# The last LayerNorm of a DiT layer: the second tile's mean taken off in PSUM by TensorE, its root by ScalarE's Sqrt and one Newton round

## The chip, the cores and the metric

The kernel runs on one core of a Trainium2 chip, in fp32 with products split into high and low parts. A core has five engines that run side by side and wait for each other through semaphores: TensorE (PE in the profile, with its weight loads as PEld), VectorE (DVE), ScalarE (ACT), GpSimd (POOL) and SyncE (SP), which here issues the DMAs. Each engine works its own instructions off in order. The metric is the device time of one execution in microseconds (us), as the median of several runs.

## What is computed

One layer of a diffusion transformer: 256 latent tokens and 256 context tokens of width 2048, two groups of attention heads, one output projection, a SwiGLU feed-forward network of width 5632, and a LayerNorm behind each of the two residual sums. Cut to its end, which is what the change concerns:

```python
def layer_norm(x, g, b):
    xf = x.astype(jnp.float32)
    mu = jnp.mean(xf, axis=-1, keepdims=True)
    var = jnp.mean(jnp.square(xf - mu), axis=-1, keepdims=True)
    return ((xf - mu) * lax.rsqrt(var + EPS) * g + b).astype(x.dtype)
...
x = layer_norm(DN_ALPHA * x + g1 * (heads @ w_out[layer]), ln1_g[layer], ln1_b[layer])
x = layer_norm(DN_ALPHA * x + g2 * swiglu(modulate(x, sh2, sc2), w_gate[layer], w_up[layer], w_down[layer]),
               ln2_g[layer], ln2_b[layer])
```

## The kernel before

The 256 latent tokens are two tiles t = 0, 1 of 128 tokens, one token to a partition. `xt[:, t, :]` holds the 2048 features of a tile, worked on in four blocks n = 0..3 of 512 columns, as wide as one PSUM bank. There are eight banks, four in the pool "acc" and four in the pool "wk".

A weight block (128 rows x 4 x 512 columns) is loaded by SP into a `raw` tile, cast by ACT into a high part `hi` (L331), and DVE subtracts to get the low part `lo` (L332). PE then does three products for every block of 128 rows (L341 to L343, `mm3`). The `hi`/`lo` pieces stand in four buffers, so ACT's next cast waits until PE has done with an older piece. Most of the kernel's order on each engine is decided by a scheduler at build time; inside `tc.manual_schedule` the code's own order holds for the named engines.

The end of the kernel is the down projection, block by block of output columns. For each block n < 3, `residual` (L1197) multiplies the sum by the gate, adds it to `xt` and takes its statistics with bn_stats (L1201). For the last block, `last_steps` (L1875) puts the gate into the last three weight groups instead (L1891, `gated`), adds what the earlier groups gave to `xt` (L1899, L1900, `seed`), copies that into a PSUM bank (L1901), and lets PE add the last three groups on top of it, for tile 0 first and then for tile 1. So the bank `whole[t]` ends up with the finished residual sum of block 3.

Then comes `ending(t, ps)` (L1833), in its own order on DVE and ACT. It takes bn_stats of the bank, calls `ln_scalars(t, True)` (L1203), which merges the four statistics (L1206) and finds one over the root of the variance: a first guess by shifting bits (L1210, L1211, L1213 on DVE) and three Newton rounds on ACT (L1216 to L1218). Meanwhile DVE takes off the mean and multiplies by the gain in all four blocks (L1826, `first_step`). When the root is there, DVE multiplies by it and adds the bias (L1830, `last_step`), and each piece goes out by a DMA on SP's queue (L1831). Tile 1's block 3 is cut into 384 and 128 columns.

Other names: `l2g` and `l2b` are the LayerNorm's gain and bias, spread over the partitions and loaded long before the end; `ident` is a 128x128 identity, `ones` a 128x128 matrix of ones, `bcol` a tile of bias columns, all three last read well before the end; `stats`, `mv` (mean, variance), `lv`, `la`, `ly` are the small tiles of the statistics.

Of the kernel before, what the change touches and what calls it, by code (L numbers as in the profile page):

```python
# [13 lines left out]
F32 = mybir.dt.float32  # L14
# [4 lines left out]
AF = mybir.ActivationFunctionType  # L19
ALU = mybir.AluOpType  # L20
# [3 lines left out]
P = 128  # L24
# [4 lines left out]
NT = SEQ // P  # L29
# [4 lines left out]
EPS = 1e-6  # L34
SCALE = HD ** -0.5
ALPHA = 2.0 ** 0.25
NB = 512
# [229 lines left out]
def dit_layer(ctx: ExitStack, tc: tile.TileContext, x, c, cx, c_ctx, w_ada, b_ada, w_in, q_norm_g,  # L267
              k_norm_g, sink_logit, w_out, ln1_g, ln1_b, w_gate, w_up, w_down, ln2_g, ln2_b,
              rope_cos, rope_sin, out):
    nc = tc.nc  # L270
    x, c, cx = x[0], c, cx[0]
    w_ada, w_in, w_out, w_gate, w_up, w_down = (w[0] for w in (w_ada, w_in, w_out, w_gate, w_up, w_down))

    main = ctx.enter_context(tc.tile_pool(name="main", bufs=1))
# [5 lines left out]
    def acc_bank():  # L280
        return acc_ps.tile([P, NB], F32, tag="acc", name="acc")

    def wk_bank():
        return wk_ps.tile([P, NB], F32, tag="wk", name="wk")
# [14 lines left out]
    ident = main.tile([P, P], F32, tag="ident", name="ident")  # L299
    make_identity(nc, ident)  # L300
    fill(main, 416)
    xt = main.tile([P, NT, D], F32, tag="xt", name="xt")
    stats = main.tile([P, NT, 4, 6], F32, tag="stats", name="stats")
# [4 lines left out]
    def load_raw(w, k0, nk, c0, width):  # L308
        raw = raw_tile()
        rv = raw[:, : nk * width]  # L310
        nc.sync.dma_start(
            rv.rearrange("p (k n) -> p k n", k=nk),
            w[k0 * P : (k0 + nk) * P, c0 : c0 + width].rearrange("(k p) n -> p k n", p=P),
        )
        return rv

    def load_split(w, k0, c0, nk=G4, width=NB, spare=False):
        return split_raw(load_raw(w, k0, nk, c0, width), spare)

    def split_raw(raw, spare=False):  # L320

        parts = []
        for s in range(0, raw.shape[-1], SUB * NB):
            n = min(SUB * NB, raw.shape[-1] - s)
            if spare:
                both = wraw.tile([P, 2, SUB * NB], F32R, tag="raw", name="hilo")
                hi, lo = both[:, 0, :], both[:, 1, :]
            else:
                hi = whl.tile([P, SUB * NB], F32R, tag="hi", name="hi")
                lo = whl.tile([P, SUB * NB], F32R, tag="lo", name="lo")  # L330
            nc.scalar.copy(hi[:, :n], raw[:, s : s + n])  # L331
            nc.vector.tensor_tensor(lo[:, :n], raw[:, s : s + n], hi[:, :n].bitcast(F32), op=ALU.subtract)  # L332
            parts += [(hi[:, j : j + NB], lo[:, j : j + NB]) for j in range(0, n, NB)]
        return parts
# [5 lines left out]
    def mm3(ps, xh, xl, w, first, last, seeded=False):  # L340
        nc.tensor.matmul(ps, lhsT=xh, rhs=w[0], start=first, stop=False, skip_group_check=seeded)  # L341
        nc.tensor.matmul(ps, lhsT=xh, rhs=w[1], start=False, stop=False, skip_group_check=seeded)  # L342
        nc.tensor.matmul(ps, lhsT=xl, rhs=w[0], start=False, stop=last, skip_group_check=seeded)  # L343
# [67 lines left out]
    ones = main.tile([P, P], F32, tag="ones", name="ones")  # L411
# [3 lines left out]
    bcol = main.tile([P, 6 * KD], F32, tag="bcol", name="bcol")  # L415
# [787 lines left out]
    def ln_scalars(t, beside=False):  # L1203

        mv = main.tile([P, 2], F32, tag="mv", name="mv", bufs=2)
        nc.vector.bn_aggr(mv, stats[:, t, :, :])  # L1206
        v = main.tile([P, 2], F32, tag="lv", name="lv", bufs=2)
        y = main.tile([P, 1], F32, tag="ly", name="ly", bufs=2)
        a = main.tile([P, 1], F32, tag="la", name="la", bufs=2)
        nc.vector.tensor_scalar_add(v[:, 0:1], mv[:, 1:2], EPS)  # L1210
        nc.vector.tensor_single_scalar(a.bitcast(I32), v[:, 0:1].bitcast(I32), 1, op=ALU.logical_shift_right)  # L1211
        (nc.scalar.mul if beside else nc.vector.tensor_scalar_mul)(v[:, 1:2], v[:, 0:1], -0.5)
        nc.vector.tensor_scalar(y.bitcast(I32), a.bitcast(I32), -1.0, float(0x5F3759DF), op0=ALU.mult, op1=ALU.add)  # L1213
        for i in range(3):
            if beside:
                nc.scalar.activation(a, y, AF.Square)  # L1216
                nc.scalar.activation(a, a, AF.Copy, bias=1.5, scale=v[:, 1:2])
                nc.scalar.activation(y, y, AF.Copy, scale=a)  # L1218
            else:
                nc.vector.tensor_scalar(a, y, y, v[:, 1:2], op0=ALU.mult, op1=ALU.mult)  # L1220
                nc.vector.tensor_scalar(y, a, 1.5, y, op0=ALU.add, op1=ALU.mult)
        return mv[:, 0:1], y

    norm = {}
# [70 lines left out]
    start = F.add("SP", 0, lambda: None, at=1e5)  # L1295
# [3 lines left out]
    for g in range(last):  # L1299
        n = GROUPS[g][1]  # L1300
# [493 lines left out]
    whole = pb.tile([P, NT, NB], F32, tag="lgb", name="hh")  # L1794
# [15 lines left out]
    l2g, l2b = l2[:, 0, :], l2[:, 1, :]  # L1810
# [13 lines left out]
    def first_step(t, n, ps):  # L1824
        sl = slice(n * NB, (n + 1) * NB)
        nc.vector.scalar_tensor_tensor(xt[:, t, sl], xt[:, t, sl] if n < 3 else ps, norm[t][0], l2g[:, sl], op0=ALU.subtract, op1=ALU.mult)  # L1826

    def last_step(t, n, s, width):
        sl = slice(n * NB + s, n * NB + s + width)
        nc.vector.scalar_tensor_tensor(xt[:, t, sl], xt[:, t, sl], norm[t][1], l2b[:, sl], op0=ALU.mult, op1=ALU.add)  # L1830
        nc.sync.dma_start(out[0, t * P : (t + 1) * P, sl], xt[:, t, sl])  # L1831

    def ending(t, ps):  # L1833
        nc.vector.bn_stats(stats[:, t, 3, :], ps)
        norm[t] = ln_scalars(t, True)
        for n in range(4):
            first_step(t, n, ps)
        for n in range(4):
            if n < 3 or t == 0:
                last_step(t, n, 0, NB)  # L1840
            else:
                last_step(t, n, 0, 3 * P)
                last_step(t, n, 3 * P, P)

    def share(n, e):

# [28 lines left out]
    def last_steps():  # L1875

        n, ng = 3, KF // G4
        sl = slice(n * NB, (n + 1) * NB)
        whole = [acc_bank() for _ in range(NT)]
        raws, ws = {}, {}  # L1880

        def mms(ps, g, t):
            for j in range(4):
                k = g * 4 + j
                mm3(ps, hTh[g][:, j, t * P : (t + 1) * P], hTl[g][:, j, t * P : (t + 1) * P], ws[g][j],
                    False, k == KF - 1 or k == (ng - TAIL) * 4 - 1, True)

        def gated(g):
            raws[g] = load_raw(w_down, g * 4, G4, n * NB, NB)
            wv = raws[g].rearrange("p (k n) -> p k n", k=G4)  # L1890
            nc.vector.tensor_mul(wv, wv, g2sb[:, None, sl].to_broadcast([P, G4, NB]))  # L1891

        def step(g):
            ws[g] = load_split(w_down, g * 4, n * NB)
            for t in range(NT):
                mms(accs[n][t], g, t)

        def seed(t):
            nc.vector.tensor_mul(yts[t], accs[n][t], g2sb[:, sl])  # L1899
            nc.vector.tensor_add(xt[:, t, sl], xt[:, t, sl], yts[t])  # L1900
            nc.scalar.copy(whole[t], xt[:, t, sl])  # L1901

        def tail():
            g0 = ng - TAIL
            gated(g0)
            step(g0 - 1)
            ws[g0] = split_raw(raws[g0])
            gated(g0 + 1)
            seed(0)
            gated(g0 + 2)  # L1910
            ws[g0 + 1] = split_raw(raws[g0 + 1])
            ws[g0 + 2] = split_raw(raws[g0 + 2], True)
            seed(1)
            for t in range(NT):
                for g in range(g0, ng):
                    mms(whole[t], g, t)
            with tc.manual_schedule(engines={ET.DVE, ET.Activation}):
                for t in range(NT):
                    ending(t, whole[t])

        return [lambda g=g: step(g) for g in range(ng - TAIL - 1) if g != FOLD_H] + [tail]

# [63 lines left out]
```

## Time and profile before

| | us |
|---|---|
| median of 3 runs | 1124.48 |
| lowest and highest run | 1122.33, 1124.83 |
| span of the profiled execution, first to last instruction | 1121.0 |
| PE's weight loads busy, share of the span | 79% |
| largest group: L341 to L343 into acc, u2h and u2l, 3 x 390 products | 456 |
| casts of weights on ACT (L331), 279 of them | 290.7 |
| low parts of weights on DVE (L332), 279 of them | 336.1 |

The profile is of one execution; it gives the span and no time outside of it, so the medians and the span are not the same measure. In its rows stand the start and the length in us, the engine, the line of the code, the operation, output and inputs by the program's names (buffer numbers left out), their shapes, and how many instructions are merged in the row; in brackets stands how long the engine had idled and what it waited for. In rows of groups the line comes first, and behind the shapes the count, the busy time in us and the mean length of one in ns.

### The profile page before, as it was taken

What the parts mean: (1) busy time and instruction counts of PE and PEld (TensorE: products, weight loads), DVE (VectorE), ACT (ScalarE), POOL (GpSimd) and SP (SyncE); (2) the same over time, 40 slices, a digit from 0 to 9 for tenths busy, and PEclk for the clock granted to TensorE, in tenths of its full rate; (3) what the DMA queues carried; (4) which work ended last, traced back from release to release, by engine and by line L of the source; (5) the groups of instructions that cost most, each with busy time, mean ns of one, the idle gap of its engine ahead of it and who ended that gap; (6) DMA issues with size and microseconds to landing.
All of it is one profiled execution on the core that took longest, in us unless ns stands there. A gap on an engine that the chain in (4) does not pass through costs nothing.

```text
span 1121.0 us, 14130 instructions
## 1 busy us (share of the span) xinstructions
PE 1102.3 (98%) x5213; PEld 883.7 (79%) x5213; DVE 903.4 (81%) x1133; ACT 598.7 (53%) x875; POOL 36.7 (3%) x82
## 2 busy tenths in 40 slices
PE   8999999999999999999999999999999999999995
PEld 6766688777887788888888878888888888888884
DVE  5763589899999888787778697988996987689876
ACT  3341554878685356444475565767766344444442
POOL 1000030110100001000000000000000000000000
PEclk9999999999999999999999999999999999999998
DMA  9999999778999778999956677777776998669742
GB/s 321 394 385 375 393 362 377 247 234 274 345 332 395 249 269 321 348 318 296 336 182 216 223 220 266 234 246 271 228 267 216 329 348 293 228 235 379 287 149 76
DMA packets 178317, 321.26 MB, mean 287 GB/s; under 512 B 8732, under 2 KB 43196, under 8 KB 175943
## 3 DMA queue, kind: packets, MB, share of 16 engines
q1 hardware_dynamic: 177528, 320.03, 81.7%
q8 instruction: 41, 0.67, 0.2%
q10 hardware_dynamic: 720, 0.33, 0.1%
q14 instruction: 28, 0.23, 0.1%
HBM read 304.07 MB, written 16.25 MB: 286 GB/s over the span
## 4 chain that ended last, share of the span: by engine, by line
PE 91%; DMA 3%; DVE 2%; ACT 1%; SPq 1%; issue 0%; ACTq 0%; DVEq 0%
PE acc L341 20%; PE acc L343 20%; PE acc L342 20%; PE wk L342 8%; PE wk L341 8%; PE wk L343 8%; PE wk L1081 2%; PE wk L654 2%; DMA raw<-in_w_in_dram 2%; DVE lo L332 1%; DMA lgb<-in_ln_g_dram 1%; PE wk L755 1%; SPq L569 1%; DMA xt<-in_x_dram 0%; PE wk L1414 0%
## 5 line engine op out<-in xcount | busy, mean ns | idle before, releaser
L331 ACT CAST hi<-raw 128x1024 fp32r<-128x1024 f32 x279 | 290.7, 1054 | 256.4 <-PE acc L343 162.4
L332 DVE TENSOR_TENSOR lo<-raw,hi 128x1024 fp32r<-128x1024 f32 x279 | 336.1, 1220 | 103.6 <-ACT hi L331 101.4
L341 PE MATMUL acc<-hi,u2h 128*128 128x512 f32 x390 | 152.5, 391 | 0.0
L343 PE MATMUL acc<-hi,u2l 128*128 128x512 f32 x390 | 151.7, 390 | 0.7 <-DVE u2l L1669 0.7
L342 PE MATMUL acc<-lo,u2h 128*128 128x512 f32 x390 | 151.8, 389 | 0.0
L603 ACT CAST hi<-raw 128x1024 fp32r<-128x1024 f32 (+1 forms) x86 | 87.4, 1030 | 113.8 <-DMA raw<-in_w_in_dram 63.2
L466 DVE SCALAR_TENSOR_TENSOR adav<-raw,cs,adav 128x512 f32<-128x512 f32 (+1 forms) x128 | 121.4, 949 | 8.4 <-DMA raw<-in_w_ada_dram 4.9
L606 DVE TENSOR_TENSOR lo<-raw,hi 128x1024 fp32r<-128x1024 f32 (+1 forms) x86 | 101.3, 1194 | 16.3 <-ACT hi L603 15.5
L341 PE MATMUL acc<-hi,uh 128*128 128x512 f32 x256 | 103.7, 405 | 1.3 <-ACT uh L769 0.8
L342 PE MATMUL wk<-lo,u2h 128*128 128x512 f32 x264 | 103.1, 390 | 0.5 <-DVE lo L332 0.5
L343 PE MATMUL wk<-hi,u2l 128*128 128x512 f32 x264 | 102.7, 389 | 0.0
L341 PE MATMUL wk<-hi,u2h 128*128 128x512 f32 x264 | 102.2, 389 | 0.0
L342 PE MATMUL acc<-lo,uh 128*128 128x512 f32 x256 | 100.5, 392 | 0.6 <-DVE lo L606 0.6
L343 PE MATMUL acc<-hi,ul 128*128 128x512 f32 x256 | 100.1, 391 | 0.4 <-DVE ul L784 0.4
L341 PE MATMUL acc<-hi,hTh 128*128 128x512 f32 x236 | 92.0, 390 | 0.4 <-ACT acc L1901 0.4
L342 PE MATMUL acc<-lo,hTh 128*128 128x512 f32 x236 | 91.8, 389 | 0.0
L343 PE MATMUL acc<-hi,hTl 128*128 128x512 f32 x236 | 91.8, 389 | 0.0
L343 PEld LDWEIGHTS acc<-hi,u2l 128*128 128x128 f32 x390 | 73.2, 188 | 16.2 <-DVE u2l L1669 1.1
L341 PEld LDWEIGHTS acc<-hi,u2h 128*128 128x128 f32 x390 | 73.2, 188 | 16.1 <-ACT u2h L1668 0.8
L342 PEld LDWEIGHTS acc<-lo,u2h 128*128 128x128 f32 x390 | 73.2, 188 | 15.1
L341 PEld LDWEIGHTS acc<-hi,uh 128*128 128x128 f32 x256 | 48.1, 188 | 19.0 <-issue 5.6
L342 PEld LDWEIGHTS wk<-lo,u2h 128*128 128x128 f32 x264 | 49.5, 188 | 12.0 <-DVE lo L332 1.8
(277 smaller groups left out, 1748.0 us busy)
## 6 DMA issues: line engine op xcount, KB each, us to landing
raw<-in_w_ada_dram SPq DMA_DIRECT2D x70, 1024.0 KB, 7.7
raw<-in_w_gate_dram SPq DMA_DIRECT2D x44, 1024.0 KB, 6.7
raw<-in_w_up_dram SPq DMA_DIRECT2D x44, 1024.0 KB, 5.6
raw<-in_w_down_dram SPq DMA_DIRECT2D x44, 1024.0 KB, 5.8
raw<-in_w_ada_dram SPq DMA_DIRECT2D x48, 512.0 KB, 5.9
raw<-in_w_in_dram SPq DMA_DIRECT2D x18, 1024.0 KB, 11.0
raw<-in_w_out_dram SPq DMA_DIRECT2D x16, 1024.0 KB, 6.5
pd<-hx SPq DMA_DIRECT2D x64, 128.0 KB, 3.4
```

What stands on the lines that cost most here:

```text
L331: nc.scalar.copy(hi[:, :n], raw[:, s : s + n])
L332: nc.vector.tensor_tensor(lo[:, :n], raw[:, s : s + n], hi[:, :n].bitcast(F32), op=ALU.subtract)
L341: nc.tensor.matmul(ps, lhsT=xh, rhs=w[0], start=first, stop=False, skip_group_check=seeded)
L342: nc.tensor.matmul(ps, lhsT=xh, rhs=w[1], start=False, stop=False, skip_group_check=seeded)
L343: nc.tensor.matmul(ps, lhsT=xl, rhs=w[0], start=False, stop=last, skip_group_check=seeded)
L466: nc.vector.scalar_tensor_tensor(a[:, c : c + piece], raw[:, f : f + piece], cs[:, 4 * (g * (G4 * NB // w) + j) + 2, None], a[:, c : c + p ...
L569: nc.sync.dma_start(room.t, w[k0 * P : (k0 + 1) * P, c0 : c0 + width])
L603: nc.scalar.copy(hl.hi[:, :n], raw.t[:, s : s + n])
L606: nc.vector.tensor_tensor(hl.lo[:, :n], raw.t[:, s : s + n], hl.hi[:, :n].bitcast(F32), op=ALU.subtract)
L654: nc.tensor.matmul(bank.t[32 * j : 32 * j + 32, :width], lhsT=cs[:, 4 * k + 2 - 2 * i : 4 * k + 34 - 2 * i], rhs=raw.t[:, c * width : (c + ...
L755: nc.tensor.transpose(ps.t[:, (j * 2 + t) * P : (j * 2 + t + 1) * P], src, ident)
L1081: nc.tensor.matmul(o_ps.t[:, : 2 * P].rearrange("p (g q) -> p g q", q=32), lhsT=v, rhs=pv[:, k], start=k == 0, stop=k == 3)
```

## The change

For tile 1, the three blocks that are finished early (n = 0, 1, 2) are multiplied by the gain ahead of time and put into three banks of the "wk" pool (`scaled_tokens`). When the mean is known, ACT makes a diagonal matrix of minus the mean (the identity was negated earlier), and PE adds minus mean times gain to each of the three banks. Only block 3 still has its mean taken off by DVE. The root comes from ACT's Sqrt with a table that is loaded earlier, a reciprocal on DVE and one Newton round there; minus half the variance is made on POOL. The last steps of the three blocks read the banks, block 3 goes first, and the cut into 384 and 128 columns moves to block 2. Tile 0 stays as it was.

```diff
-    def last_step(t, n, s, width):
+    def last_step(t, n, s, width, src=None):
         sl = slice(n * NB + s, n * NB + s + width)
-        nc.vector.scalar_tensor_tensor(xt[:, t, sl], xt[:, t, sl], norm[t][1], l2b[:, sl], op0=ALU.mult, op1=ALU.add)
+        src = xt[:, t, sl] if src is None else src[:, s : s + width]
+        nc.vector.scalar_tensor_tensor(xt[:, t, sl], src, norm[t][1], l2b[:, sl], op0=ALU.mult, op1=ALU.add)
         nc.sync.dma_start(out[0, t * P : (t + 1) * P, sl], xt[:, t, sl])
...
         for n in range(4):
-            if n < 3 or t == 0:
-                last_step(t, n, 0, NB)
-            else:
-                last_step(t, n, 0, 3 * P)
-                last_step(t, n, 3 * P, P)
+            last_step(t, n, 0, NB)
+
+    eps = bcol[:, 0:1]
+
+    def scaled_tokens(t):
+        res = [wk_bank() for _ in range(3)]
+        for n, q in enumerate(res):
+            nc.vector.tensor_mul(q, xt[:, t, n * NB : (n + 1) * NB], l2g[:, n * NB : (n + 1) * NB])
+        nc.scalar.mul(ident, ident, -1.0)
+        nc.gpsimd.memset(eps, EPS)
+        nc.scalar.activation(bcol[:, 1:2], stats[:, t, 2, 2:3], AF.Sqrt, bias=eps)
+        return res
+
+    def last_ending(t, ps, scaled):
+        mv, lv, ly, la = (main.tile([P, w], F32, tag=c, name=c, bufs=2) for c, w in (("mv", 2), ("lv", 2), ("ly", 1), ("la", 1)))
+        nc.vector.bn_stats(stats[:, t, 3, :], ps)
+        nc.vector.bn_aggr(mv, stats[:, t, :, :])
+        nc.gpsimd.tensor_scalar(lv[:, 0:1], mv[:, 1:2], -0.5, -0.5 * EPS, op0=ALU.mult, op1=ALU.add)
+        nc.scalar.activation(ones, ident, AF.Copy, scale=mv[:, 0:1])
+        nc.scalar.activation(lv[:, 1:2], mv[:, 1:2], AF.Sqrt, bias=eps)
+        for n, q in enumerate(scaled):
+            nc.tensor.matmul(q, lhsT=ones, rhs=l2g[:, n * NB : (n + 1) * NB], start=False, stop=True, skip_group_check=True)
+        norm[t] = mv[:, 0:1], ly
+        first_step(t, 3, ps)
+        nc.vector.reciprocal(ly, lv[:, 1:2])
+        nc.vector.tensor_scalar(la, ly, ly, lv[:, 0:1], op0=ALU.mult, op1=ALU.mult)
+        nc.vector.tensor_scalar(ly, la, 1.5, ly, op0=ALU.add, op1=ALU.mult)
+        last_step(t, 3, 0, NB)
+        for n in range(2):
+            last_step(t, n, 0, NB, scaled[n])
+        last_step(t, 2, 0, 3 * P, scaled[2])
+        last_step(t, 2, 3 * P, P, scaled[2])
...
             seed(1)
+            scaled = scaled_tokens(1)
             for t in range(NT):
                 for g in range(g0, ng):
                     mms(whole[t], g, t)
             with tc.manual_schedule(engines={ET.DVE, ET.Activation}):
-                for t in range(NT):
-                    ending(t, whole[t])
+                ending(0, whole[0])
+                last_ending(1, whole[1], scaled)
```

In the changed file L1830 has become L1831, L1848 to L1850 have become L1878 to L1880, and L1891 has become L1921.

What stands on DVE at the very end, behind tile 0's last steps. Before:

```order
L1834 BN_STATS stats<-acc 128x6
L1206 BN_AGGR mv<-stats 128x2
L1210 TENSOR_SCALAR lv<-mv 128x1
L1211 TENSOR_SCALAR la<-lv 128x1
L1213 TENSOR_SCALAR ly<-la 128x1
L1826 SCALAR_TENSOR_TENSOR xt<-xt,mv,l_7593 128x512 x3
L1826 SCALAR_TENSOR_TENSOR xt<-acc,mv,l_7593 128x512
L1830 SCALAR_TENSOR_TENSOR xt<-xt,ly,l_7593 128x512 x3
L1830 SCALAR_TENSOR_TENSOR xt<-xt,ly,l_7593 128x384
L1830 SCALAR_TENSOR_TENSOR xt<-xt,ly,l_7593 128x128
```

And with the change (l_7593 is the tile of gain and bias):

```order
L1857 BN_STATS stats<-acc 128x6
L1858 BN_AGGR mv<-stats 128x2
L1826 SCALAR_TENSOR_TENSOR xt<-acc,mv,l_7593 128x512
L1866 RECIPROCAL ly<-lv 128x1
L1867 TENSOR_SCALAR la<-ly,lv 128x1
L1868 TENSOR_SCALAR ly<-la,ly 128x1
L1831 SCALAR_TENSOR_TENSOR xt<-xt,ly,l_7593 128x512
L1831 SCALAR_TENSOR_TENSOR xt<-wk,ly,l_7593 128x512 x2
L1831 SCALAR_TENSOR_TENSOR xt<-wk,ly,l_7593 128x384
L1831 SCALAR_TENSOR_TENSOR xt<-wk,ly,l_7593 128x128
```

Three first steps and the bit guess are gone from DVE, the reciprocal and the Newton round have come to it, and four of the last steps read banks that PE writes. ACT's ten instructions for tile 1 are replaced by two (L1860, L1861) at the same place, and PE has three products (L1863) behind its last L343.

The multiplications that fill the banks stand on DVE among the low parts of the weights, during the down projection of the last block. The first stands some 14 rows earlier, behind the last `lo<-adav`; this is where the other two went:

```order
-L1850 TENSOR_TENSOR xt<-xt,room 128x512 x2
+L1880 TENSOR_TENSOR xt<-xt,room 128x512 x2
+L1847 TENSOR_TENSOR wk<-xt,l_7593 128x512
+L332 TENSOR_TENSOR lo<-raw,hi 128x1024 x2
+L1847 TENSOR_TENSOR wk<-xt,l_7593 128x512
+L332 TENSOR_TENSOR lo<-raw,hi 128x1024 x2
+L1921 TENSOR_TENSOR raw<-raw,room 128x2048
```

Two multiplications have come between the sums of block 3 and the low parts that follow.

The early Sqrt with its table load stands on ACT among the casts of the same stretch, behind the last copy of a gate row (L480):

```order
 L331 CAST hi<-raw 128x1024 x2
 L480 COPY room<-wk 128x512
-L331 CAST hi<-raw 128x1024 x15
+L331 CAST hi<-raw 128x1024 x4
+L1850 ACT_TABLE_LOAD
+L1850 ACTIVATE bcol<-stats,bcol 128x1
+L331 CAST hi<-raw 128x1024 x11
```

The load and the Sqrt have come behind the fourth of fifteen casts; the Sqrt reads the statistics of tile 1's block 2 and so waits for DVE's second L1201, and eleven casts stand behind it.

## The prediction

> **What bounds the kernel now.** I read the page's busy table and its chain shares first, then the chain of waits in order of time, then the timeline of the last 15 us, engine by engine.
>
> ```profile
> PE 1102.3 (98%) x5213; PEld 883.7 (79%) x5213; DVE 903.4 (81%) x1133; ACT 598.7 (53%) x875; POOL 36.7 (3%) x82
> PE 91%; DMA 3%; DVE 2%; ACT 1%; SPq 1%; issue 0%; ACTq 0%; DVEq 0%
> ```
>
> TensorE (PE) is the bound of the whole kernel. The change adds work to it only behind its last product, so the 98% says one thing: whatever is added to other engines earlier costs nothing unless it starves PE. What can be won lies behind PE's last product, which the end of the chain of waits shows:
>
> ```profile
> 1109.99 0.24 PE acc L343
> 1110.26 0.71 DVE stats L1834
> 1110.99 0.28 DVE mv L1206
> ...
> 1114.19 0.30 ACT ly L1218
> 1114.52 0.75 DVE xt L1830
> ```
>
> PE is done at 1110.23. From there to the span's end at 1121.0 are 10.8 us, in which VectorE (DVE) and ScalarE (ACT) normalise the second tile and the output DMAs drain. The same stretch in the timeline:
>
> ```profile
> 1111.29 0.15 DVE L1210 TENSOR_SCALAR lv<-mv 128x1 f32<-128x1 f32 x1
> 1111.47 0.20 ACT L1212 ACTIVATE lv<-lv 128x1 f32<-128x1 f32 x1 [5.14 <-DVE lv L1210]
> ...
> 1111.73 2.07 DVE L1826 SCALAR_TENSOR_TENSOR xt<-xt,mv,l 128x512 f32<-128x512 f32 x3
> 1113.72 0.74 DVE L1826 SCALAR_TENSOR_TENSOR xt<-acc,mv,l 128x512 f32<-128x512 f32 x1
> 1114.52 2.87 DVE L1830 SCALAR_TENSOR_TENSOR xt<-xt,ly,l 128x512 f32<-128x512 f32 x5
> 1115.30 2.69 SPq L1831 DMA_DIRECT2D out_dram<-xt  x5
> ```
>
> Two chains run side by side and end together. DVE does four first steps (L1826) until 1113.72 + 0.74 = 1114.46. ACT does three Newton rounds, whose last row in the chain ends at 1114.19 + 0.30 = 1114.49. The last steps (L1830) start at 1114.52 and end at 1114.52 + 2.87 = 1117.39; the queue of output DMAs follows them, and 1121.0 - 1117.39 = 3.6 us pass from the last DVE instruction to the end. Shortening one of the two chains alone would give nothing. The change shortens both.
>
> **The new chain behind the last product.** The statistics (1110.26) and their merge (1110.99) stay; the first instruction that needs the mean starts at 1111.29, as L1210 does now, and a result of DVE reaches ACT 0.03 later (1111.29 + 0.15 to 1111.47). The removed instructions are three L1826, L1210, L1211, L1213 and ten ACT ones. From 1111.29 on three things start at once.
>
> DVE does the one remaining L1826: 1111.29 + 0.74 = 1112.03.
>
> ACT makes the matrix with minus the mean on its diagonal (128x128, pointer scale), then the Sqrt (128x1, pointer bias):
>
> ```profile
> L873 ACT ACTIVATE sq<-kvacc 128x128 bf16<-128x128 f32 x8 | 2.4, 309 | 0.0
> L1666 ACT ACTIVATE uf<-wk,mB,mA 128x128 f32<-128x128 f32 x8 | 3.2, 453 | 8.2 <-PE wk L1445 8.2
> L1217 ACT ACTIVATE la<-la,lv 128x1 f32<-128x1 f32 x6 | 1.8, 295 | 0.2
> L1216 ACT ACTIVATE la<-ly 128x1 f32<-128x1 f32 x6 | 1.2, 203 | 0.5 <-DVE ly L1213 0.3
> ```
>
> The matrix lies between 0.31 (128x128 without a pointer) and 0.45 (with two pointers and from PSUM). I take 0.31 plus what a pointer adds at 128x1, 0.295 - 0.203 = 0.09: 0.40, so it ends at 1111.69. The Sqrt is taken as L1217, 0.30, end 1111.99; with 0.03 to DVE it is there at 1112.02, just as DVE comes free. Sqrt itself is not in this trace; its bounds are the 0.20 and 0.45 of these rows.
>
> GpSimd (POOL) makes minus half the variance:
>
> ```profile
> 385.68 0.20 POOL L1129 TENSOR_TENSOR mB<-mB,sh 128x4 f32<-128x4 f32 x1
> 209.03 1.27 POOL L362 TENSOR_SCALAR rs_t<-rs_t 128x8 f32<-128x8 f32 x1
> ```
>
> Small POOL instructions take 0.20 when nothing disturbs them and up to 1.27 when something does. I take 0.20, ready at about 1111.5. It is first wanted by L1867 at 1112.22 (below), so it has 0.7 us of cover; at 1.27 it is ready at 1112.6 and costs 0.4.
>
> Then DVE does the reciprocal and one Newton round. The trace has all three forms, the last two in the LayerNorm 1 code:
>
> ```profile
> L1053 DVE RECIPROCAL ll<-ll 128x2 f32<-128x2 f32 x16 | 2.5, 159 | 0.8 <-ACT pr L1043 0.5
> 377.57 0.28 DVE L1220 TENSOR_SCALAR la<-ly,lv 128x1 f32<-128x1 f32 x1
> 377.88 0.21 DVE L1221 TENSOR_SCALAR ly<-la,ly 128x1 f32<-128x1 f32 x1
> 378.14 0.27 DVE L1220 TENSOR_SCALAR la<-ly,lv 128x1 f32<-128x1 f32 x1
> ```
>
> From start to start the round takes 0.31 and 0.26, and the reciprocal 0.16 + 0.03 = 0.19. So: reciprocal 1112.03, L1867 1112.22, L1868 1112.53, first of the last steps at 1112.79. That is 1114.52 - 1112.79 = **1.73 us** earlier.
>
> The last steps are five as before and of the same sizes, four full banks' worth with the last one cut into 384 and 128 columns.
>
> ```profile
> 1106.36 2.74 DVE L1830 SCALAR_TENSOR_TENSOR xt<-xt,ly,l 128x512 f32<-128x512 f32 x4
> ```
>
> Four of 0.75 in 2.74 are one every (2.74 - 0.75) / 3 = 0.665, so in the new chain they start at 1112.79, 1113.45, 1114.12 and 1114.79, and the pair of pieces then takes 2.87 - 3 x 0.665 = 0.875. Three of them read PSUM banks: L1826 takes 0.74 from PSUM as from SBUF in the rows above, so no extra.
>
> **Do the banks come in time?** The second, third and fourth of those wait for TensorE's three products (L1863), in full fp32. The same form, ones times a 128x512 fp32 operand, is in the trace:
>
> ```profile
> 338.05 0.42 PEld L485 LDWEIGHTS wk<-g1b,ones 128*128 128x128 f32 x2
> 339.34 0.59 ACT L486 COPY g1b<-wk 128x512 f32<-128x512 f32 x1 [0.33 <-PE wk L485]
> 340.20 0.59 ACT L486 COPY g1b<-wk 128x512 f32<-128x512 f32 x1 [0.27 <-PE wk L485]
> ```
>
> From the first weight load to the reader of the first bank are 339.34 - 338.05 = 1.29, and each further bank takes 340.20 - 339.34 = 0.86. With weights at 1111.69 + 0.03 = 1111.72 the banks are ready at 1113.01, 1113.87 and 1114.73, against 1113.45, 1114.12 and 1114.79. All three are in time, the last by only 0.06. So bank and scalar chain end together again, and the end moves from 1117.39 to 1114.79 + 0.875 = 1115.67, by **1.7 us**.
>
> That holds only at full clock, and PE now pauses from 1110.23 to 1111.72:
>
> ```profile
> 266.50:270.00 3.50, 2.21 (x11) 1.00 0.44 120
> 1108.50:1112.00 3.50, 1.72 (x8) 1.00 0.64 247
> 1112.50:1113.00 0.50, 0.00 (x0) 0.90 0.00 0
> 1113.00:1113.50 0.50, 0.00 (x0) 0.50 0.00 0
> ```
>
> The fourth column is the granted clock: it halved at about 1112.9, 2.7 us after the last product, and did not where PE was busy for 2.21 of 3.50 us. The 3.5 us that end at 1112.9 held 1110.23 - 1109.4 = 0.8 us of work; with the new products they hold another 1.0 to 1.1, 1.9 in all, between those two cases and nearer the one that kept its clock. I take full clock. The Trainium skill ("TensorE: Matmul & The Clock Gate", section "What's actually happening") says that the clock halves after at least one idle window of about 3.4 us, and that these windows run freely. By that a pause of 1.5 us costs nothing and the sum stays; by the row, where 2.7 us of idling sufficed, a window with some work in it can also trip.
>
> **What is added earlier.** Three multiplications (L1847, at most 0.74 each, taken as L1826), a table load with a small Sqrt on ACT, a negation of the identity (0.31, as L873) on an ACT that is busy for 53% of the span, and a memset of one column on a POOL that is busy for 3%.
>
> ```profile
> L1581 ACT ACT_TABLE_LOAD x1 | 1.3, 1283 | 0.0
> 1055.12 1.06 ACT L331 CAST hi<-raw 128x1024 fp32r<-128x1024 f32 x1 [0.30 <-PE acc L343]
> 1058.06 0.69 DVE L1201 BATCH_NORM_STATS2 stats<-xt 128x6 f32<-128x512 f32 x1
> 1059.20 1.06 ACT L331 CAST hi<-raw 128x1024 fp32r<-128x1024 f32 x1 [3.02 <-PE acc L343]
> 1060.56 1.06 ACT L331 CAST hi<-raw 128x1024 fp32r<-128x1024 f32 x1 [0.30 <-PE acc L343]
> 1060.99 2.35 DVE L332 TENSOR_TENSOR lo<-raw,hi 128x1024 fp32r<-128x1024 f32 x2
> 1064.64 1.05 ACT L331 CAST hi<-raw 128x1024 fp32r<-128x1024 f32 x1 [3.02 <-PE acc L343]
> 1065.72 2.59 DVE L332 TENSOR_TENSOR lo<-raw,hi 128x1024 fp32r<-128x1024 f32 x2 [2.38 <-ACT hi L331]
> ```
>
> By the order the load and the small Sqrt stand behind the cast of 1055.12. The load runs from 1056.18 to 1057.5, in 3.02 us in which ACT waits for PE anyway. The Sqrt waits for L1201, 1058.06 + 0.69 = 1058.75, and is over by about 1059.1; behind it stand eleven casts, the first of which could not start before 1059.20. Two of the multiplications stand in DVE's run after 1058 and make its lo products up to 1.5 later, which the 2.38 us of idling before 1065.72 swallow. Does PE feel it? A group of weights is worked off in 1064.64 - 1059.20 = 5.44 us, and the cast of 1059.20 fills the first half of the group after next: it is wanted 1.36 + 5.44 = 6.8 later, at 1066.0, and its lo is done at about 1062.2. Cover 3.8, used 1.5: nothing.
>
> **Sum.** The profiled span of 1121.0 becomes 1119.3. The median of the runs, 1124.48, stands 3.5 above that span, and I carry the same difference over: 1124.48 - 1.7 = **1122.8 us**, -0.15%. About 0.2%, or 2.25 us, is what a measurement of this kernel can tell from no change, so the likeliest result is a true gain that doesn't count as one.
>
> **Rivals.**
> 1. The clock halves at the time it did before, 1112.9. The first bank (1113.01) is nearly through; the others take 2 x 0.86 = 1.72: 1114.73 and 1116.45. The pieces end at 1116.45 + 0.875 = 1117.33, a gain of 0.1: **1124.4**. For it: the share of work in the window is unproven. Against: 266.50. Chance 0.09.
> 2. Slower: the clock halves before the products start. All six passes take double: 1.29 + 0.86 = 2.15 to the first bank, 1.72 for each other, so 1113.87, 1115.59, 1117.31, end 1118.19, 0.8 later: **1125.3**. It decides once the third bank is later than 1116.5. Against: the full clock until 1112.5. Chance 0.04.
> 3. Slower beyond the 0.2%: ACT's casts are held by the small Sqrt, or DVE's lo products by L1847, until PE starves around 1066. It decides at 3.8 us of delay; to be slower by 2.25 net of the gain it needs 3.8 + 1.7 + 2.25 = 7.8 us, **1126.7** and more. The rows give 1.5. Chance 0.05.
> 4. The end is held by the output DMAs, which move at their own pace, or POOL is slow (0.4): gain 1.3 or less, **1123.2** to 1124. For it: the five DMAs follow each other without a gap. Against: they follow DVE's steps and shift with them. Chance 0.07.
>
> **Numbers.** The forecast has 0.75. With every lower bound (ACT's matrix 0.31, Sqrt 0.20) the gain is 1.9, with the upper ones (0.45 and 0.45) 1.5; so by mechanism 1122.6 to 1123.0. Runs scatter more than that: the three of before lie from 1122.33 to 1124.83, and their median is near the top. That carries about 0.29 of the forecast past the 0.2% line; the rest, and rivals 1, 2 and 4, fall within it: 0.46 + 0.20 = 0.66. Slower: rival 3, 0.05. The range goes from 1122.33 less 1.7, about 1120.8, up past rival 1 to 1124.9; rivals 2 and 3 are left out.
>
> **What the profile after would show.** The first last step starts 1112.79 - 1110.99 = 1.8 us after the merge of the statistics (3.5 before); three products in two passes each, 0.43 apart; no gap ahead of the fourth last step (a gap of 0.3 or more says that PE is late: clock); granted clock 1.00 to their end; ACT's table load inside a wait for PE and PE's last product at the same time to within the scatter. A PE end that is microseconds later, or gaps on PE after 1050 that were not there, would make the prediction wrong, and so would a fourth last step later than 1116.

## The result, and the profile after

| | before | changed |
|---|---|---|
| median of 22 runs, us | 1122.38 | 1120.68 |
| lowest and highest | 1120.38, 1124.83 | 1119.63, 1122.72 |
| span of the profiled execution | 1121.0 | 1119.6 |
| ratio of the times | | 0.9983, 95% interval 0.9976 to 0.9990 |

The change takes off 0.17% (0.10 to 0.24), or 1.9 us (1.1 to 2.7); the medians differ by 1.70 us. That is clear of zero and smaller than the 0.2% that a measurement of this kernel can tell from no change. The forecast gain was 1.7 us. The forecast time was not right: 1122.8 with a range from 1120.8 stands against 1120.68, though the runs of before moved just as much, from a median of 1124.48 in the three runs known then to 1122.38 in 22.

The end of the kernel on DVE, in the timeline of the changed kernel (start, length in us, line, operation, output and inputs):

```profile
1110.53 0.70 DVE L1857 BATCH_NORM_STATS2 stats<-acc 128x6 f32<-128x512 f32 x1 [1.15 <-PE acc L343]
1111.26 0.26 DVE L1858 BATCH_NORM_AGGREGATE mv<-stats 128x2 f32<-128x24 f32 x1
1111.56 0.75 DVE L1826 SCALAR_TENSOR_TENSOR xt<-acc,mv,l 128x512 f32<-128x512 f32 x1
1112.23 0.15 DVE L1866 RECIPROCAL ly<-lv 128x1 f32<-128x1 f32 x1
1112.49 0.27 DVE L1867 TENSOR_SCALAR la<-ly,lv 128x1 f32<-128x1 f32 x1
1112.80 0.21 DVE L1868 TENSOR_SCALAR ly<-la,ly 128x1 f32<-128x1 f32 x1
1113.05 0.75 DVE L1831 SCALAR_TENSOR_TENSOR xt<-xt,ly,l 128x512 f32<-128x512 f32 x1
1113.72 2.19 DVE L1831 SCALAR_TENSOR_TENSOR xt<-wk,ly,l 128x512 f32<-128x512 f32 x4
```

From the merge (1111.26) to the first last step (1113.05) are 1.79 us; the sum had 1.80, and before it was 3.53. The four last steps that read banks follow without a gap, so the banks come in time: the third is through at about 1112.02 + 2.84 = 1114.86, and its reader, the first of the two pieces, starts 0.87 before DVE's end at 1115.91, at 1115.04. The same stretch on the other three engines:

```profile
1110.11 0.39 PE L343 MATMUL acc<-hilo,hTl 128*128 128x512 f32 x1
1112.02 2.84 PE L1863 MATMUL wk<-l,ones 128*128 128x512 f32 x6 [1.52 <-ACT ones L1860]
...
1111.56 0.40 ACT L1860 ACTIVATE ones<-ident,mv 128x128 f32<-128x128 f32 x1 [4.96 <-DVE mv L1858]
1111.87 0.28 ACT L1861 ACTIVATE lv<-mv,bcol 128x1 f32<-128x1 f32 x1
...
1111.62 0.19 POOL L1859 TENSOR_SCALAR lv<-mv 128x1 f32<-128x1 f32 x1 [90.98 <-DVE mv L1858]
```

Each of the terms that were bounded before is near the value taken: the matrix 0.40 (0.40), the Sqrt 0.28 (0.30), POOL's instruction 0.19 (0.20), PE's pause 1.52 (1.49). The granted clock, in the stretch of the products and where it fell (columns: stretch, width, PE busy, clock, DMA share, GB/s):

```profile
1109.40:1112.90 3.50, 1.98 (x7) 1.00 0.47 180
1112.00:1115.00 3.00, 2.84 (x6) 1.00 0.11 42
1119.00:1119.50 0.50, 0.00 (x0) 0.51 0.05 16
```

It held through the products and fell at about 1119.0. The early part, in the timeline of ACT:

```profile
1055.44 1.06 ACT L331 CAST hi<-raw 128x1024 fp32r<-128x1024 f32 x1 [0.30 <-PE acc L343]
1056.51 1.28 ACT L1850 ACT_TABLE_LOAD   x1
1059.10 0.29 ACT L1850 ACTIVATE bcol<-stats,bcol 128x1 f32<-128x1 f32 x1 [1.30 <-DVE stats L1201]
1059.56 1.05 ACT L331 CAST hi<-raw 128x1024 fp32r<-128x1024 f32 x1 [0.17 <-PE acc L343]
```

The load lies inside what had been 3.02 us of waiting for PE; the Sqrt waits for the statistics as expected, and the cast behind it still waits for PE, by 0.17 us. On DVE the wait ahead of the next low parts, 2.38 us before, is now 1.21, so the multiplications have used up half of it:

```profile
1066.09 2.54 DVE L332 TENSOR_TENSOR lo<-raw,hi 128x1024 fp32r<-128x1024 f32 x2 [1.21 <-ACT hi L331]
```

Below, the **tail** is the time from the start of PE's last L343 to the end of the span. It was 1121.0 - 1109.83 = 11.17 us and is now 1119.6 - 1110.11 = 9.49 us: 1.68 us gained where 1.7 were forecast.

### The profile page after: what moved, and what is told of

Same layout as the page of the kernel before. It is cut to its first block, busy times and chain, and to the rows that moved or that the text cites. A ratio compares the mean times of both kernels' runs of the same rounds, so it can differ in the third digit from the quotient of the medians.

```text
span 1119.6 us, 14141 instructions
## 1 busy us (share of the span) xinstructions
PE 1104.5 (99%) x5219; PEld 884.7 (79%) x5219; DVE 903.6 (81%) x1133; ACT 598.0 (53%) x870; POOL 39.2 (3%) x84
## 4 chain that ended last, share of the span: by engine, by line
PE 90%; DMA 5%; ACT 2%; DVE 2%; SPq 0%; issue 0%; ACTq 0%; DVEq 0%
PE acc L341 20%; PE acc L343 20%; PE acc L342 20%; PE wk L342 8%; PE wk L341 8%; PE wk L343 8%; DMA raw<-in_w_in_dram 4%; PE wk L1081 2%; PE wk L654 2%; DMA raw<-in_w_out_dram 1%; ACT hi L603 1%; DMA pd<-hx 1%; PE wk L755 0%; DMA xt<-in_x_dram 0%; DVE lo L606 0%; PE wk L1414 0%
## 5 line engine op out<-in xcount | busy, mean ns | idle before, releaser
L343 PE MATMUL acc<-hi,u2l 128*128 128x512 f32 x390 | 151.8, 390 | 0.7 <-DVE u2l L1669 0.7
L343 PE MATMUL wk<-hi,u2l 128*128 128x512 f32 x264 | 102.7, 389 | 0.0
L343 PE MATMUL acc<-hi,ul 128*128 128x512 f32 x256 | 100.1, 391 | 0.4 <-DVE ul L784 0.4
L343 PE MATMUL acc<-hi,hTl 128*128 128x512 f32 x236 | 91.9, 389 | 0.0
L343 PEld LDWEIGHTS acc<-hi,u2l 128*128 128x128 f32 x390 | 73.2, 188 | 16.3 <-DVE u2l L1669 1.1
L341 PEld LDWEIGHTS wk<-hi,u2h 128*128 128x128 f32 x264 | 49.6, 188 | 10.4
```

## Experiments

Each kernel was timed beside the kernel before. Ratios are of times against it, with their 95% interval where there were enough runs. The diffs are against the changed kernel, with `...` where lines are left out. Each trace is of one execution.

### Only the new root

Tile 1's mean is taken off by DVE as before; the root is Sqrt, reciprocal and one round.

```diff
-        res = [wk_bank() for _ in range(3)]
...
+        res = []
...
-        for n, q in enumerate(scaled):
-            nc.tensor.matmul(q, lhsT=ones, ...)
...
         first_step(t, 3, ps)
         nc.vector.reciprocal(ly, lv[:, 1:2])
         nc.vector.tensor_scalar(la, ly, ly, lv[:, 0:1], op0=ALU.mult, op1=ALU.mult)
         nc.vector.tensor_scalar(ly, la, 1.5, ly, op0=ALU.add, op1=ALU.mult)
...
+        for n in range(3):
+            first_step(t, n, ps)
...
```

> Measure: the tail, from the start of PE's last L343 to the end of the span: 1121.0 - 1109.83 = 11.17 us before, 1119.6 - 1110.11 = 9.49 us with the change. Here only the root is made in the new way (Sqrt, reciprocal, one Newton round, variance half on POOL); the mean is taken off by DVE in four first steps as before, no banks, no products. Theory A (two chains that end together, DVE's and ACT's): DVE now carries four first steps and the reciprocal with its round, so the last steps start 4 x 0.665 + 0.76 = 3.4 us after the first first step, against 3.23 from 1111.29 to 1114.52 before: tail 11.2 to 11.5, no gain or a small loss. Rival B (ACT's three rounds alone set the end): the gain of the change comes with the root, tail 9.4 to 9.8.

Measured: median 1122.49 (1120.84 to 1125.18), ratio 0.9998 (0.9987 to 1.0008). DVE's timeline at the end:

```profile
1112.64 0.75 DVE L1826 SCALAR_TENSOR_TENSOR xt<-acc,mv,l 128x512 f32<-128x512 f32 x1
1113.31 0.15 DVE L1858 RECIPROCAL ly<-lv 128x1 f32<-128x1 f32 x1
...
1114.01 2.07 DVE L1826 SCALAR_TENSOR_TENSOR xt<-xt,mv,l 128x512 f32<-128x512 f32 x3
1116.00 2.86 DVE L1831 SCALAR_TENSOR_TENSOR xt<-xt,ly,l 128x512 f32<-128x512 f32 x5
```

The last steps start 1116.00 - 1112.64 = 3.36 us after the first instruction that needs the mean (3.23 before, from L1210 at 1111.29), the tail is 1122.5 - 1111.19 = 11.31 us. The root was ready at 1114.1, and nothing was won. Theory A holds, rival B falls.

### Only the new mean

The banks and the products are there, the root comes from three rounds on ACT.

```diff
         nc.scalar.activation(ones, ident, AF.Copy, scale=mv[:, 0:1])
-        nc.scalar.activation(lv[:, 1:2], mv[:, 1:2], AF.Sqrt, bias=eps)
+        nc.vector.tensor_scalar_add(v[:, 0:1], mv[:, 1:2], EPS)
...
+        for i in range(3):
+            nc.scalar.activation(a, y, AF.Square)
+            nc.scalar.activation(a, a, AF.Copy, bias=1.5, scale=v[:, 1:2])
+            nc.scalar.activation(y, y, AF.Copy, scale=a)
-        nc.vector.reciprocal(ly, lv[:, 1:2])
...
```

> Only the mean is taken off in the new way (three banks, three products, one first step on DVE); the root is made by three Newton rounds on ACT as before, with the diagonal matrix ahead of them. Theory A: ACT's rounds end at 1114.49 in the trace of before, or up to 0.2 later as the matrix stands ahead, and the last steps wait for them: tail 11.1 to 11.5 us. Rival C (DVE's four first steps alone set the end): the gain comes with the banks, tail 9.4 to 9.8.

Measured: median 1122.10 (1120.91 to 1126.84), ratio 0.9996 (0.9983 to 1.0010). DVE's timeline:

```profile
1111.75 0.74 DVE L1826 SCALAR_TENSOR_TENSOR xt<-acc,mv,l 128x512 f32<-128x512 f32 x1
1114.53 0.75 DVE L1831 SCALAR_TENSOR_TENSOR xt<-xt,ly,l 128x512 f32<-128x512 f32 x1 [2.04 <-ACT ly L1863]
```

The three first steps that DVE no longer does have become 2.04 us of waiting for ACT. The tail is 1121.1 - 1109.84 = 11.26 us. Theory A holds, rival C falls. It is the tails that say so, as the interval of the times has the change's 0.17% at its edge: each half alone gains nothing there, both together 1.68 us.

### Only what is added early

```diff
     def last_ending(t, ps, scaled):
-        mv, lv, ly, la = ...
         nc.vector.bn_stats(stats[:, t, 3, :], ps)
...
+        norm[t] = ln_scalars(t, True)
+        for n in range(4):
+            first_step(t, n, ps)
...
```

The banks are filled and not read.

> All that the change adds early (three multiplications into banks, table load, small Sqrt, negation, memset), with the end as before; the banks are not read. Theory A: hidden, so PE needs the same time from its last L478 (1049.12 in the trace of before) to the start of its last L343 (1109.83): 60.71 us, to within 0.1 (60.67 in the trace of the change, from 1049.44 to 1110.11), and the tail is 11.2; time against before 1.000. Rival D (the early part costs something): PE needs 0.2 us or more longer there, or the time is above before by the same.

Measured: median 1122.08 (1121.29 to 1126.75), ratio 0.9990 (0.9980 to 1.0000). The profiled execution was a long one, of span 1125.0, yet from its last L478 (1053.08 in its chain) to the start of its last L343 (1113.75) passed 60.67 us, against 60.71 before and 60.67 in the change, and its tail is 11.25 us. The early part costs nothing that shows, and rival D falls. So a span can be 4 us longer with the same last 72 us. Not all that is added lies in that stretch: the first multiplication starts at 1046.49 in the trace of the change, the negation of the identity at 582.0, the memset at 12.9. From PE's first L1473 (a transposition, at 432.7 there) to its last L478 pass 616.7 us in the change and 616.5 here, against 618.0 before and 616.5 in a second execution of it, so the negation shows no cost either.

### Twice the products

```diff
-        nc.scalar.mul(ident, ident, -1.0)
+        nc.scalar.mul(ident, ident, -0.5)
...
         for n, q in enumerate(scaled):
-            nc.tensor.matmul(q, lhsT=ones, ...)
+            for _ in range(2):
+                nc.tensor.matmul(q, lhsT=ones, ...)
```

> The change with each of the three products done as two with half the mean, so PE takes twice as long for the banks, as it would at half its clock. Theory A with the banks just in time: the banks come 0.86, 1.72 and 2.6 us later than in the change, the pair of pieces waits for the third one, the tail grows by 2.4 to 2.6 us, to about 12.0, slower than before by 0.8: the price that the second rival of the prediction had. Rival E (the banks have room to spare of a microsecond or more): the tail grows by less than 1.6.

Measured, in one execution: 1123.77, span 1121.9, last L343 at 1110.28, so a tail of 11.62 us. PE and DVE:

```profile
1112.19 5.42 PE L1864 MATMUL wk<-l,ones 128*128 128x512 f32 x12 [1.52 <-ACT ones L1860]
...
1114.21 0.75 DVE L1831 SCALAR_TENSOR_TENSOR xt<-wk,ly,l 128x512 f32<-128x512 f32 x1 [0.24 <-PE wk L1864]
1115.93 0.75 DVE L1831 SCALAR_TENSOR_TENSOR xt<-wk,ly,l 128x512 f32<-128x512 f32 x1 [0.96 <-PE wk L1864]
1117.64 0.88 DVE L1831 SCALAR_TENSOR_TENSOR xt<-wk,ly,l 128x384 f32<-128x384 f32 x2 [0.97 <-PE wk L1864]
```

DVE now waits for each bank. Its last step ends 1118.52 - 1110.28 = 8.24 us after the start of the last L343, against 1115.91 - 1110.11 = 5.80 in the change: 2.44 later, as theory A had it. The products took 5.42 - 2.84 = 2.58 us longer, so the third bank had 2.58 - 2.44 = 0.14 us to spare in the change. The tail grew by only 11.62 - 9.49 = 2.13, short of the 2.4 to 2.6 expected, and is 0.45 above that of before, where the second rival of the prediction had 0.8. From DVE's end to the span's end are 3.38 us here and 3.69 in the change, so the output DMAs have caught up by 0.3 (see the part on them below).

### A longer pause of PE

```diff
+        nc.scalar.copy(bcol[:, 2:3], mv[:, 1:2])
+        for _ in range(11):
+            nc.scalar.copy(bcol[:, 2:3], bcol[:, 2:3])
         nc.scalar.activation(ones, ident, AF.Copy, scale=mv[:, 0:1])
```

> The change with twelve dependent one-column copies on ACT ahead of the diagonal matrix (about 0.23 us each, 2.8 in all), so PE's pause between its last L343 and the first of its three products grows from 1.5 to about 4.3 us. In the trace of before the granted clock halved 2.7 us after the last product, in that of the change it stayed at 1.00 to the end. Theory F (a pause of 2.7 us or more lets the clock fall): the clock is 0.50 when the products start, their six passes stand 0.86 apart and take some 5.4 us from first start to last end, and the tail is 9.49 + 2.8 + 2.5 = 14.8. Rival G (it falls only after a longer rest, or when a running window happens to end): clock 1.00, 0.43 apart, 2.84 in all as in the change, tail 12.3.

Measured, in one execution: 1125.95, span 1124.2, last L343 at 1109.92, tail 14.28 us. PE's timeline, then its clock by stretches:

```profile
1114.37 5.49 PE L1866 MATMUL wk<-l,ones 128*128 128x512 f32 x6 [4.07 <-ACT ones L1863]
...
1113.20:1113.70 0.50, 0.00 (x0) 0.58 0.00 0
1114.20:1114.70 0.50, 0.33 (x1) 0.50 0.00 0
1119.70:1120.20 0.50, 0.16 (x1) 0.59 0.75 295
```

After 3.0 us of rest the clock halved (58% of full as the mean of that half microsecond, so at about 1113.3), and the six passes took 5.49 us instead of 2.84. In this execution the numbers are those of theory F. The tail is 0.5 shorter than expected, about half of it because the copies were done in 2.55 us rather than 2.8; the DMAs' 0.3 as above and the 0.14 that the third bank had to spare make up the rest, less 0.15 by which the products took longer than expected.

As a rule, theory F does not hold. The same rows from the traces of "only the new root" (last product over at 1111.58), "only what is added early" (1114.14) and "the kernel before once more" (1110.46):

```profile
1116.00:1116.50 0.50, 0.00 (x0) 0.97 0.00 0
1116.00:1116.50 0.50, 0.00 (x0) 0.82 0.00 0
1110.00:1121.00 11.00, 0.46 (x3) 0.68 0.35 131
```

By the means, the clock halved at about 1116.5, 1116.3 and 1114.0, which is 4.9, 2.2 and 3.5 us after the last product. So 2.7 us of rest does not always suffice, and the moment changes from execution to execution, as rival G's second half had it. One execution shows what a halved clock costs, not how often this kernel would meet it.

### No Newton round

```diff
         nc.vector.reciprocal(ly, lv[:, 1:2])
-        nc.vector.tensor_scalar(la, ly, ly, lv[:, 0:1], op0=ALU.mult, op1=ALU.mult)
-        nc.vector.tensor_scalar(ly, la, 1.5, ly, op0=ALU.add, op1=ALU.mult)
```

> The change without the Newton round and without minus half the variance on POOL: the reciprocal of ACT's Sqrt is the root. Left out: the correction of the Sqrt's error. The last steps could start 0.31 + 0.26 = 0.57 us earlier. Theory A with the banks just in time (third bank 0.06 us ahead of its reader): the pair of pieces waits for the third bank and most of it is lost, tail 9.2 to 9.5. Rival E (the banks have room): the whole 0.57 is won, tail 8.9.

Measured: median 1119.46 (1118.79 to 1120.91), ratio 0.9974 (0.9962 to 0.9986). DVE's timeline:

```profile
1110.73 0.75 DVE L1831 SCALAR_TENSOR_TENSOR xt<-xt,ly,l 128x512 f32<-128x512 f32 x1
1111.49 2.59 DVE L1831 SCALAR_TENSOR_TENSOR xt<-wk,ly,l 128x512 f32<-128x512 f32 x4
```

The four steps that read banks take 2.59 us instead of 2.19, and the first of them comes 0.09 later than it could: DVE waits for the banks. Its end moves by only 5.80 - (1114.08 - 1108.42) = 0.14 us, as theory A had it, and as much as the third bank had to spare by the run with twice the products. The tail, 1117.5 - 1108.42 = 9.08, fell by 0.41, below the 9.2 to 9.5 expected and short of rival E's 8.9, so neither range was met. The output DMAs started 0.6 earlier, and a third bank that is late holds them up by less than it holds DVE.

### No Newton round, products in one pass

```diff
-        nc.scalar.activation(ones, ident, AF.Copy, scale=mv[:, 0:1])
+        nc.scalar.activation(onesr, ident, AF.Copy, scale=mv[:, 0:1])
...
-            nc.tensor.matmul(q, lhsT=ones, rhs=l2g[:, n * NB : (n + 1) * NB], start=False, ...)
+            nc.tensor.matmul(q, lhsT=onesr, rhs=gr[n], start=False, ...)
```

`gr[n]` is the gain of block n, rounded to fp32r by ACT ahead of time.

> As e6, with the three products in one pass: the diagonal and the gain are rounded to fp32r, the gain by three early casts on ACT. Left out: the correction of the Sqrt's error, and the low part of mean times gain. Theory A: the banks come at 0.23 instead of 0.86 us each, so the scalar chain alone sets the end: the last steps start 0.57 us earlier and follow each other without a gap, tail 8.9, and the time is below before by about 0.2% (2.3 us). Rival D: three more casts or the shorter chain show no gain, tail 9.3 or more.

Measured: median 1120.60 (1117.91 to 1123.39), ratio 0.9982 (0.9973 to 0.9990). PE and DVE, then PE's clock:

```profile
1114.63 0.96 PE L1869 MATMUL wk<-l2gr,onesr 128*128 128x512 f32 x3 [1.52 <-ACT onesr L1866]
...
1115.03 0.75 DVE L1831 SCALAR_TENSOR_TENSOR xt<-xt,ly,l 128x512 f32<-128x512 f32 x1
1115.70 2.19 DVE L1831 SCALAR_TENSOR_TENSOR xt<-wk,ly,l 128x512 f32<-128x512 f32 x4
...
1112.40:1115.90 3.50, 1.66 (x7) 1.00 0.36 137
1115.50:1116.00 0.50, 0.09 (x1) 0.90 0.00 0
1116.00:1116.50 0.50, 0.00 (x0) 0.50 0.00 0
```

Three products take 0.96 us instead of 2.84, there is no gap, and the tail is 1121.5 - 1112.72 = 8.78 us, as theory A had it (8.9): the shortest of all, 0.71 below the change. The times do not show it: their interval has the expected 0.2% in it, as well as the change's 0.17%. Rival D falls by its tail of 9.3 or more. Whether this one or the last is the fastest by time stays open, since runs of one kernel scatter by more than the 0.3 us between their tails.

### The kernel before once more

The kernel is unchanged, so there is no edit.

> The kernel before, unchanged, for its time beside its span. In 22 runs of the changed kernel the time was the run's span plus 1.79 to 1.87 us. Theory H (the time is the span plus 1.8 for this kernel too, and the three runs that stood beside the prediction lay high in the scatter): every run here is its span plus 1.8 to 1.9, the median lies near 1122.4, and PE's time from its last L478 to its last L343 and the tail are those of the first trace (60.71 and 11.2 us), whatever the span. Rival I (before has some 3.5 us outside of its span): time minus span is 3 or more.

Measured: median 1122.11 (1120.91 to 1125.19), ratio to the other runs of the same kernel 0.9997 (0.9987 to 1.0006). In its ten runs the time is 1.74 to 2.05 us above the span; the profiled one took 1123.13 with a span of 1121.3, so 1.83. Rival I falls. Theory H holds in the main: its 1.8 to 1.9 is too narrow, as five of the ten lie above it and two below, and over all 65 executions of this kernel beside the experiments the difference is 1.74 to 2.13 us. The tail is 1121.3 - 1110.07 = 11.23 us. What differs between these executions lies ahead of the last L478:

| kernel | first L1081 | last L478 | last L343 | L478 to L343 | span |
|---|---|---|---|---|---|
| before | 232.1 | 1049.12 | 1109.83 | 60.71 | 1121.0 |
| before again | 232.3 | 1049.41 | 1110.07 | 60.66 | 1121.3 |
| changed | 233.0 | 1049.44 | 1110.11 | 60.67 | 1119.6 |
| only early part | 236.8 | 1053.08 | 1113.75 | 60.67 | 1125.0 |
| no Newton round | 231.7 | 1047.75 | 1108.42 | 60.67 | 1117.5 |
| one pass | 233.8 | 1052.04 | 1112.72 | 60.68 | 1121.5 |

The spans lie 7.5 us apart, 2.2 of which are the tails. Of the 5.3 us between the earliest and the latest last L478, 5.1 are there by 232 to 237 us; but the one-pass execution is 0.8 behind the changed one at that point and 2.6 at its last L478, so some is lost behind it too. All edits but a memset and a few single ACT instructions lie behind 1046 us. What the executions wait for differently ahead of that stays open.

## Why the prediction was right and wrong

**What bounds the end: right.** Two chains that end together were the base of the sum. Each half of the change alone left the tail at 11.3 us, both together made it 9.49 (11.17 and 11.23 before).

**The new chain: right.** 1.80 us from the merge to the first last step was the sum, 1.79 the measurement, and no term was off by more than 0.1. That the two agree to 0.01 is luck: the first step held DVE for 0.67 rather than 0.74, the reciprocal for 0.26 rather than 0.19, and these cancel. The gain of DVE's end is (1117.39 - 1109.83) - 5.80 = 1.76 us (1.7 forecast). The 1.9 that the prediction gave for its lower bounds does not follow from its terms: with ACT faster, DVE would still have been busy with its one first step until 1112.03, and the gain would have stayed at 1.7.

**Banks just in time: right.** There is no gap in the change, and the third bank had 0.14 us to spare, where the sum had 0.06; with 0.57 taken off the scalar chain the banks did become the bound, and with one pass they stopped being it.

**The early part: right, it costs nothing.** The 60.7 us of PE from its last L478 are unchanged, and the early part alone left the time where it was (0.9980 to 1.0000).

**The clock: the value taken was right, its reason shown in part.** Before, a stretch of 3.5 us with 0.8 us of work let the clock fall; in the changed kernel one with 1.98 did not; in the one-pass kernel one with 1.66 did. But the work in the last 3.5 us does not settle it: in the changed kernel the clock was still full at 1119.0, with no work since 1114.86. The Trainium skill ("TensorE: Matmul & The Clock Gate", section "What's actually happening") has it fall after at least one idle window of about 3.4 us. The runs differ: 3.0 us of rest sufficed with the longer pause and 2.2 with only the early part, and in the one-pass kernel it fell 0.3 us after the last product, with 0.96 us of products in the 2.8 before. By the rule the first rival could not happen; by these rows a kernel with a little less work of PE might meet it. The 22 runs of the changed kernel did not, but for the last microsecond of the products at most: their mean granted clock is 0.998 to 1.000 (0.997 in the run with the longer pause). At 0.998 the clock was halved for some 5.6 us at most, by an estimate from that rounded mean, and the last 4.7 us of the span lie behind the products.

**The output DMAs: a rival that was half right.** They do shift with DVE's steps, as written against it, but only with the first: from there on they move at a pace of their own. Half microseconds of before (two), of the change (two) and of the kernel without a Newton round; the last two columns are the DMA share and GB/s:

```profile
1116.50:1117.00 0.50, 0.00 (x0) 0.50 1.00 373
1118.00:1118.50 0.50, 0.00 (x0) 0.50 1.00 365
1115.10:1115.60 0.50, 0.00 (x0) 1.00 0.98 365
1116.60:1117.10 0.50, 0.00 (x0) 1.00 1.01 368
1113.50:1114.00 0.50, 0.00 (x0) 1.00 0.72 266
```

DVE hands over 256 KB every 0.665 us, which is 394 GB/s, and the DMA engines, full all the time, move 365 to 389. So they fall behind by a little, and catch up where the steps have gaps and the share drops: from DVE's end to the span's end pass 3.6 to 3.7 us in the first case and 3.4 in the second (twice the products, longer pause, no Newton round). That fits the tail without a Newton round, which fell by 0.41 though DVE's end moved by 0.14; no run changed the DMAs alone. The rival's price, a gain of 1.3 or less, did not come, as the change brings the first last step forward by 1.74 us.

**The level: wrong, and this is the step that failed.** "The median of the runs, 1124.48, stands 3.5 above that span, and I carry the same difference over." The span was of one execution and the median of three runs, and the 3.5 was carried over as if it were time outside of the span. No run with a span on record has more than 2.13 outside of it (before again: 1.74 to 2.05), so the profiled execution should have taken 1122.7 to 1123.1; its own time is not on record. Two of the three shown runs were higher up in a scatter of 1120.4 to 1124.8. The forecast missed by 2.1 us, and the median of before fell by as much, from 1124.48 to 1122.38 in 22 runs: the whole miss is the level, none of it the gain. Counted from the execution that the sum was made on, with the 1.8 that the changed kernel's runs have outside of their spans, the forecast would have been 1121.0 - 1.7 + 1.8 = 1121.1, 0.4 above the measured median. The text saw that the three runs' median was "near the top" and used it for the chances, not for the time. The lower end of the range has a slip besides: "1122.33 less 1.7" is 1120.6, not 1120.8, and 1120.68 lies between the two.

**The chances** put 0.66 on a change within 0.2%; 0.17% it was (0.10 to 0.24).

## What to carry to other kernels

Where two engines' chains end together, shorten both in one change: here each alone gave nothing and both gave 1.7 us. Add a predicted gain to the time of the execution whose span was read, or to a median of many runs, never to a few runs' median that belongs to other executions; and judge a change to the end of a kernel by its tail in the trace, which repeated here to 0.1 us in two executions of the kernel before, while spans scattered by several. Where TensorE is to come back for a short burst after its last long one, count how long it rests and how much it did: a rest of 4.1 us, with the clock halved 3.0 us into it, cost a factor of two, and rests of 1.5 us cost the products behind them nothing. Between these, the moment at which the clock falls differs from execution to execution.

## What the runs showed of the hardware

TensorE's clock can fall right behind a short burst: at 1115.9 in the one-pass kernel, 2.8 us after the long work ended, although 0.96 us of products lay in between. Behind long work alone it fell 2.2 (only the early part), 2.7 (before), 3.0 (longer pause), 3.5 (before again) and 4.9 us (only the new root) after the last product; in the changed kernel, behind its own three products, 4.1 us after them (1119.0 against 1114.86). Once halved, it stayed so through the 5.5 us of products in the run with the longer pause and was back at full only as they ended (about 1120.1).

A 128x512 product in full fp32 takes two passes and 0.86 us at full clock: 12 passes took 5.42 us and 6 took 2.84, so three products more cost 2.58. In fp32r three of them took 0.96 us in all.
